# Hybrid encoder layer on one core: block sums, token loads and residual adds are queued in other places

## The chip, the cores and the metric

The kernel is one program on one core of a Trainium2 chip. The metric is the device time of one execution in microseconds (us). The median of three runs before the change is 2272.96 us (2271.06 to 2276.23).

## What is computed

One inference step of a hybrid encoder layer, for 2048 prompt tokens and 32 sample tokens, all in float32, with 1024 model columns and 4096 hidden columns:

```
n = rmsnorm(x);  z = n @ w_in                        # one combined projection
A = windowed attention with sinks, 8 query heads     # half of the width
B = gated linear attention (GLA), 4 heads            # other half
h = x + concat(A, B) @ w_out
y = h + relu(rmsnorm(h) @ w_up)^2 @ w_down
```

It returns y and the new caches and states.

## The kernel before

The program runs four stages one after the other: attention (to about 375 us), GLA (to about 705 us), the output projection (to about 912 us) and the feed-forward part (FFN, to the end). Every float32 operand of a matmul is split into a high and a low part (names end in h and l), and each product of two splits is three matmuls. SyncE (SP) issues all DMAs; each engine works off its own list of instructions in order, and a recording layer with an estimated clock sets that order when the program is built. Generators that are spawned beside a stage (`spawn`) take their places in it by the numbers that they yield, in ns of that clock.

**FFN.** The tokens lie in three pieces of two groups each (328 columns a group in piece 0, 356 in pieces 1 and 2), taken in the order 1, 2, 0 (`ORDER`). A piece is done in 16 blocks of 256 hidden columns. Up and down projections use Strassen-Winograd, so that a block has seven up products (`u`, operands B11, B21, T2, T1, T3, B22, T4) and seven down products (`dn`), which alternate on TensorE. The token operands of a piece are made in the projection stage, stored to memory (`Td`), and loaded by `load_tok` (L1487) when the piece before has used that operand for the last time, about one operand in 3.9 us. `load_tok` loads float32 into the low tile (names T1l and so on), ScalarE copies it to the high tile (T1h), and VectorE or GpSimd subtracts. After each up product ScalarE and VectorE make the operands of the down products (uB11, uB22, uT1, ..., each h and l). `post` of a down product, in `down` (L1569), adds it from PSUM to the accumulators `P` of that piece (VectorE, L1496). Before the first block `residual` (L1606) loads h (`yd`) into accumulators 2, 3, 4 and 5, so that the first block adds onto it as well; accumulators 1, 6 and 7 are written by ScalarE copies. At a piece's end GpSimd merges accumulators (L1594), SP stores them to `out_yT`, and the next piece takes the same tiles. The weights' splits are made up to six steps ahead (`AHEAD`) from tiles named stage, which rotate in a pool of five.

**Block sums of w_down.** The FFN needs, for each of the 16 blocks, four sums of quarters of w_down (`sd`). GpSimd makes them beforehand (L712): blocks 0 to 3 beside attention (in 16 units of 128 columns, in two generators), blocks 4 to 9 beside GLA (1 MB each, in one tile), the rest in the projection by `begin`, `more` and `end`. `down_sums` (L721) loads a unit, yields 6000, sums with a pause after each sum, yields 6000 and stores.

**Output projection.** It goes over six groups (piece, half) in order, loads the residual x of a group as y (`load_y`, pools opy0 to opy2 by turns), loads the mixed heads as m and splits them into mx0 (h by ScalarE, l by GpSimd, L1113), adds (L1271), keeps a sum of squares (`acc`, matmul `oprb`), and hands the group to `post` (L1191), whose two parts run during the next group at f = 1 and 2 (for the last group, inside the FFN's first up products). `post` scales the group, for the second half also forms the Winograd sums T1 to T4, and stores all to Td.

Of the kernel before, what the change touches and what calls it, by code (L numbers as in the profile page):

```python
# [9 lines left out]
F32 = mybir.dt.float32  # L10
F32R = mybir.dt.float32r
I32 = mybir.dt.int32
AF = mybir.ActivationFunctionType
ALU = mybir.AluOpType
# [5 lines left out]
P = 128  # L20
# [6 lines left out]
ORDER = (1, 2, 0)  # L27
EARLY, MIDDLE = 4, 6
AHEAD = 6
# [33 lines left out]
class Builder:  # L63
# [230 lines left out]
    def attention_phase(self):  # L294
# [3 lines left out]
        with ExitStack() as ctx:  # L298
# [337 lines left out]
            for i, t in enumerate(order):  # L636
# [13 lines left out]
                if i == 3:  # L650
                    early = [(b, c0, P) for b in range(EARLY) for c0 in range(0, 512, P)]
                    one = lambda name: self.mid.tile([P, 576], F32, tag="cc", name=name)
                    for j in range(2):
                        self.spawn(self.down_sums(early[j::2], one, 1, 3500), 13000 * j)
                if t == nt - 1:
# [65 lines left out]
    def down_sums(self, units, tile_, parts, step):  # L721

        for b, c0, n in units:
            raw = tile_(f"sd{b}_{c0}")[:, : 4 * n].rearrange("p (k m n) -> p k m n", k=2, m=2)
            self.load_block(raw, b, c0, n)
            yield 6000
            for _ in self.block_sums(raw, parts):
                yield step
            yield 6000
            with self.tc.issue_after(self.Q.last.ins):  # L730
                self.Q.dma_start(self.sd[b][:, :, c0 : c0 + n], raw.rearrange("p k m n -> p (k m) n"))

    def prepare_gla(self, part):
# [66 lines left out]
    def gla_phase(self):  # L800
        tc, a, V, S, G, Q = self.tc, self.a, self.V, self.S, self.G, self.Q
        nt = self.nt
        with ExitStack() as ctx:
# [274 lines left out]
            whole = lambda name: sums.tile([P, 2048], F32, tag="sd", name=name)  # L1078
            self.spawn(self.down_sums([(b, 0, 512) for b in range(EARLY, EARLY + MIDDLE)], whole, 2, 4500), 4000)
            for _ in gates(0):  # L1080
# [76 lines left out]
    def op_phase(self, pool):  # L1157
# [6 lines left out]
        mmem = [[m0.tile([P, KB * REST], F32R, tag=x, name=f"mx0{x}") for x in "hl"], mem1]  # L1164
        yps = [pool(f"opy{i}", 1) for i in range(3)]
        tp, sp, xp = pool("opt", 1), pool("ops", 2), pool("opx", 2)
        stage = lambda name, n: tp.tile([P, H * REST], F32, tag="t", name=name)[:, : H * n].rearrange("p (k t) -> p k t", k=H)
# [23 lines left out]
        def post(p, gi, acc, t3):  # L1191
# [17 lines left out]
            if gi == 0:  # L1209
                for f in range(KB):  # L1210
                    scaled(y[:, f], f)
                    if f == H - 1:
                        Q.dma_start(Td["B11"], y[:, :H])
                Q.dma_start(Td["B21"], y[:, H:])
                return
# [3 lines left out]
            for k in range(H):  # L1219
# [6 lines left out]
                S.activation(y0[:, k], B, AF.Copy)  # L1226
                tt(y0[:, H + k], y0[:, H + k], B)
            for x, src in (("T2", y0[:, :H]), ("T4", y0[:, H:]), ("T1", y[:, :H]), ("T3", t3), ("B22", y[:, H:])):
                Q.dma_start(Td[x], src)
# [11 lines left out]
        def begin(b):  # L1241

            x = xp.tile([P, 2048], F32, tag="x", name=f"sd{b}").rearrange("p (k m n) -> p k m n", k=2, m=2)
            self.load_block(x, b, 0, 512)
            sums[b] = x, self.block_sums(x)
# [12 lines left out]
        for j, (p, gi) in enumerate(groups):  # L1258
# [3 lines left out]
            for f in range(KB):  # L1262
# [18 lines left out]
                if f == KB - 1:  # L1281
                    if gi:
                        Q.dma_start(self.yd[p][gi][:, :H], z)
                    Q.dma_start(self.yd[p][gi][:, H:], y[:, H:])
                if f in (1, 2) and pending is not None:
                    next(pending, None)
# [9 lines left out]
    def ffn_phase(self):  # L1296
# [4 lines left out]
        with ExitStack() as ctx:  # L1301
# [18 lines left out]
            umem |= {x: upair(uc, x) for x in ("T1", "T3", "T2", "B21")}  # L1320
            amem = {1: mem(pool("acc1"), H * NM, "P1", F32)}
            tmem |= tok(pool("tokd"), ("B11", "B21"))
            wfc = pool("wfc")
            amem |= {i: mem(pool(f"acc{i}"), H * NM, f"P{i}", F32) for i in (3, 5, 7, 6, 2, 4)}
            umem["T4"] = upair(pool("ud"), "T4")
            wfb, xa, sx = pool("wfb"), pool("xa", bufs=2), pool("sx")
# [160 lines left out]
            def load_tok(e, x, engs):  # L1487

                h, l = e.T[x]
                Q.dma_start(f32(l), self.Td[e.p][x])  # L1490
                for i, eng in enumerate(engs):
# [77 lines left out]
            def down(g, i):  # L1569
# [7 lines left out]
                for j in range(0, H, 2):  # L1577
# [5 lines left out]
                    for d in to:  # L1583
                        at = e.acc[d][:, j : j + 2]
                        if b or q not in (1, 6, 7):
                            add(at, at, ps)
                        else:
                            S.activation(at, ps, AF.Copy)

# [6 lines left out]
            def store(e, q):  # L1596

                gi, f0 = {2: (0, 0), 3: (1, 0), 4: (0, H), 5: (1, H)}[q]
                for f in range(H):
                    rows, off = slice((f0 + f) * P, (f0 + f + 1) * P), 0  # L1600
                    for t, t0, t1 in e.joined[gi]:
                        dst = self.o["yT_sample"][rows] if t == nt else self.o["yT_prompt"][rows, t0:t1]
                        Q.dma_start(dst, e.acc[q][:, f, off : off + t1 - t0])
                        off += t1 - t0

            def residual(g, i):  # L1606

                n, b = divmod(g, NF)
                if b or i not in (0, 1, 4, 5):
                    return  # L1610
                q = DOWN[i + 1][2]
                gi, f0 = {2: (0, 0), 3: (1, 0), 4: (0, H), 5: (1, H)}[q]
                Q.dma_start(envs[n].acc[q], self.yd[envs[n].p][gi][:, f0 : f0 + H])

# [5 lines left out]
            for x, g, i in steps:  # L1620
# [6 lines left out]
                else:  # L1627
                    residual(g, i)
                    down(g, i)
                    n, b = divmod(g, NF)  # L1630
                    e, end = envs[n], n + 1 == len(envs)
                    if b == NF - 2 and i == 2:
                        merge(e, 3, 5, False)
# [147 lines left out]
```

## Time and profile before

| | |
|---|---|
| median of 3 runs | 2272.96 us |
| the profiled execution | 2273.91 us, span 2272.1 us |
| TensorE busy | 2150.4 us (95%) |
| VectorE, ScalarE, GpSimd busy | 1560.5, 1231.3, 1433.5 us |
| DMA | 372.65 MB, mean 164 GB/s over the span |
| granted TensorE clock, mean | 0.972 |

TensorE is idle for 122 us of the span, and the profile's other views tell where: the waits view names the engine and line that ended each idle stretch, the timeline gives single instructions with start and duration, and the critical chain goes back from the end through whatever released each step. "SPq" rows are DMA issues on SP's queue; their duration is that of the issue, not of the transfer.

### The profile page before, as it was taken

The page shows a single profiled execution, that of the slowest core. Times are in us where ns is not written, and L with a number is a line of the kernel's source. Part 1 is how long each engine was busy: PE and PEld are TensorE (multiplying, and loading weights), DVE is VectorE, ACT ScalarE, POOL GpSimd, SP SyncE. Part 2 cuts the span into 40 slices and gives each one's busy share as a digit, 9 for nine tenths or more (in the row PEclk, how much of TensorE's full clock was granted, in tenths as well). Part 3 has the DMA queues.
Part 4 walks back from the last instruction along what each step waited for, and adds up shares of the span by engine and source line. Part 5 has one row for each costly group of instructions (what it writes and reads, how often), then busy time and mean ns, then how long its engine had stood idle before and what let it go on. Part 6 is the DMA issues. An engine that isn't in the chain of part 4 may idle for free.

```text
span 2272.1 us, 40454 instructions
## 1 busy us (share of the span) xinstructions
PE 2150.4 (95%) x14790; PEld 2018.8 (89%) x14790; DVE 1560.5 (69%) x3442; ACT 1231.3 (54%) x2728; POOL 1433.5 (63%) x1292
## 2 busy tenths in 40 slices
PE   7999999999986899699999997999999989999997
PEld 6777777888776899699999997999999979999996
DVE  8766766799984346567777775566666656776677
ACT  4555555656562122565556565655566646666662
POOL 5243345344351652577777789777777887887784
PEclk9999999999999899799999999999999989999998
DMA  7344563325146897633433358344433584344433
GB/s 265 131 156 144 182 221 132 136 73 193 61 160 191 292 324 260 240 128 127 134 126 127 121 181 311 128 129 128 132 123 121 187 283 144 122 142 133 147 109 118
DMA packets 207145, 372.65 MB, mean 164 GB/s; under 512 B 42961, under 2 KB 136450, under 8 KB 201570
## 3 DMA queue, kind: packets, MB, share of 16 engines
q1 hardware_dynamic: 206946, 370.07, 48.7%
q8 instruction: 116, 1.90, 0.3%
q14 instruction: 83, 0.68, 0.1%
HBM read 275.03 MB, written 94.98 MB: 163 GB/s over the span
## 4 chain that ended last, share of the span: by engine, by line
PE 53%; POOL 2%; DVE 2%; DMA 1%; issue 1%; ACT 0%; SPq 0%; POOLq 0%; DVEq 0%; ACTq 0%
PE dn L156 27%; PE u L156 26%; DVE P L1496 1%; POOL P L1594 1%; DMA out_yT_prompt<-P 0%; POOL wf_d0S L1378 0%; DMA T3l<-Td0T 0%; DMA T1l<-Td2T 0%; DVE P L1594 0%; POOL wf_u1S L1378 0%; DVE u L1496 0%; DMA P<-yd 0%; POOL B22l L1494 0%; POOL wf_d15S L1378 0%; POOL T3l L1494 0%
## 5 line engine op out<-in xcount | busy, mean ns | idle before, releaser
L1496 DVE TENSOR_TENSOR P<-P,dn 128x712 f32<-128x712 f32 (+1 forms) x666 | 580.9, 875 | 261.5 <-PE dn L156 227.3
L43 ACT ACTIVATE u<-u 128x356 f32<-128x356 f32 (+1 forms) x384 | 174.2, 454 | 37.3 <-PE u L156 23.5
L43 ACT ACTIVATE r<-u 128x356 f32<-128x356 f32 (+1 forms) x192 | 88.5, 461 | 138.5 <-PE u L156 138.5
L712 POOL TENSOR_TENSOR sd<-sd 128x128 f32<-128x128 f32 (+2 forms) x136 | 107.0, 806 | 88.4 <-DMA sd<-in_w_down 83.8
L1496 DVE TENSOR_TENSOR u<-u,r 128x356 f32<-128x356 f32 (+1 forms) x144 | 75.7, 525 | 121.5 <-PE u L156 103.1
L944 POOL TENSOR_TENSOR E<-cc 128x256 f32<-128x256 f32 (+1 forms) x117 | 69.5, 629 | 105.7 <-DVE cc L796 52.7
L1403 POOL TENSOR_TENSOR stage<-stage 128x512 f32<-128x512 f32 x92 | 119.3, 1297 | 23.8 <-DMA stage<-in_w_up 17.3
L1020 DVE COPY_PREDICATED AT<-masks,A 64x64 f32<-64x64 int32 (+1 forms) x330 | 82.7, 252 | 18.5 <-ACT AT L43 8.8
L1594 POOL TENSOR_TENSOR P<-P,P 128x712 f32<-128x712 f32 (+1 forms) x38 | 65.2, 1752 | 21.8 <-DVE P L1496 21.6
L43 ACT ACTIVATE P<-S,negm 128x192 f32<-128x192 f32 (+2 forms) x128 | 51.5, 416 | 47.8 <-DVE negm L577 36.7
L1271 DVE TENSOR_TENSOR y<-op,y 128x356 f32<-128x356 f32 (+1 forms) x48 | 23.6, 516 | 74.8 <-PE op L156 63.0
L43 ACT ACTIVATE E<-E 128x1024 f32<-128x1024 f32 (+2 forms) x68 | 67.2, 1012 | 1.1
L595 POOL TENSOR_TENSOR P<-P,es 128x512 f32<-128x512 f32 x15 | 15.6, 1043 | 77.2 <-ACT sq L43 33.8
L43 ACT ACTIVATE v<-go 128x256 f32<-128x256 f32 (+1 forms) x34 | 12.8, 380 | 75.7 <-DVE Sp L1052 44.5
L955 DVE TENSOR_TENSOR E<-E,kq 128x256 f32<-128x256 f32 (+1 forms) x117 | 51.4, 491 | 1.4 <-ACT E L43 1.4
L576 DVE TENSOR_REDUCE mx<-S 128x2 f32<-128x384 f32 (+2 forms) x64 | 32.7, 535 | 28.1 <-PE S L156 27.8
L43 ACT ACTIVATE op<-y 128x356 f32<-128x356 f32 (+1 forms) x42 | 18.7, 463 | 61.1 <-DVE y L1271 61.0
L1496 DVE TENSOR_TENSOR u<-u,f 128x356 f32<-128x356 f32 (+1 forms) x96 | 49.8, 519 | 2.0 <-ACT u L43 2.0
L43 ACT ACTIVATE pS<-pT 128x256 f32<-128x256 f32 (+1 forms) x62 | 27.2, 490 | 43.8 <-PE pT L160 43.8
L844 POOL TENSOR_TENSOR g<-g,ggla 128x512 f32<-128x512 f32 (+1 forms) x17 | 22.6, 1344 | 40.3 <-ACT g L43 40.3
L43 ACT ACTIVATE f<-u 128x356 f32<-128x356 f32 (+1 forms) x96 | 43.7, 455 | 0.0
L156 PEld LDWEIGHTS A<-E 64*64 64x64 f32 (+1 forms) x1704 | 32.5, 147 | 6.7 <-issue 4.7
(1911 smaller groups left out, 8756.6 us busy)
## 6 DMA issues: line engine op xcount, KB each, us to landing
stage<-sd SPq DMA_DIRECT2D x92, 512.0 KB, 4.5
stage<-in_w_up SPq DMA_DIRECT2D x92, 512.0 KB, 4.2
stage<-in_w_down SPq DMA_DIRECT2D x46, 512.0 KB, 3.6
stage<-su SPq DMA_DIRECT2D x30, 512.0 KB, 3.3
sd<-in_w_down SPq DMA_DIRECT2D x24, 512.0 KB, 6.1
sd<-sd SPq DMA_DIRECT2D x12, 1024.0 KB, 7.6
stage<-in_w_down SPq DMA_DIRECT2D x46, 256.0 KB, 3.0
xT1a<-in_xT_prompt SPq DMA_DIRECT2D x16, 512.0 KB, 4.3
```

Source lines behind the costliest of these rows:

```text
L43: ins = f(*args, **kw)
L156: self._pe(self.T.matmul(out, lhsT, rhs, start=start, stop=stop, **kw), ns)
L576: V.reduce_max(mx[:, ch, us], sp, axis=AX.X)
L712: self.G.tensor_tensor(out=o, in0=x, in1=y, op=op)
L844: G.tensor_tensor(out=gv, in0=gv, in1=ggla[:r].unsqueeze(1).broadcast_to([r, 4, P]), op=ALU.mult)
L944: G.tensor_tensor(out=e4, in0=c4, in1=ref, op=ALU.subtract)
L955: V.tensor_tensor(out=e4, in0=e4, in1=halves_of(kq, L, m), op=ALU.mult)
L1020: V.copy_predicated(dst, mk.unsqueeze(1).broadcast_to([L // nh, 2, w // m, m]), src[r].rearrange("s p (n m) -> s p n m", m=m),)
L1271: V.tensor_tensor(out=y[:, f], in0=ps, in1=y[:, f], op=ALU.add)
L1403: tt = lambda o, x, y, op: G.tensor_tensor(out=o, in0=x, in1=y, op=op)
L1496: add = lambda out, x, y, op=ALU.add: V.tensor_tensor(out=out, in0=x, in1=y, op=op)
L1594: eng.tensor_tensor(out=e.acc[q][:, j : j + 2], in0=e.acc[q][:, j : j + 2], in1=e.acc[x][:, j : j + 2], op=ALU.add)
```

## The change

- `EARLY, MIDDLE` goes from 4, 6 to 5, 5: five blocks' sums are made beside attention and five beside GLA. Their pauses are 2500 for 3500 and 3500 for 4500, the second generator starts at 14000 for 13000, and after a unit's store `down_sums` yields 8000 before it loads the next one.
- In the projection the pool opx (sums) has three larger tiles instead of two, and opy0, the pool of the first group's y, is reserved after it, so that it lies over other memory: that of GLA's sums tile.
- `post` yields once more before it stores to Td, so that the stores come some steps later.
- `load_tok` issues its DMA from ScalarE's queue instead of SP's.
- The first block no longer adds onto a loaded h in accumulators 2 to 5: VectorE copies the product there (L1592 of the changed kernel). h comes later: in blocks 2 to 9 of each piece one slice of 128x712 is loaded into a stage tile and GpSimd adds it after VectorE's own add of that block.
- The FFN's memory pools stand in another order.

```diff
-EARLY, MIDDLE = 4, 6
+EARLY, MIDDLE = 5, 5
...
             with self.tc.issue_after(self.Q.last.ins):
                 self.Q.dma_start(self.sd[b][:, :, c0 : c0 + n], raw.rearrange("p k m n -> p (k m) n"))
+            yield 8000
...
-        yps = [pool(f"opy{i}", 1) for i in range(3)]
-        tp, sp, xp = pool("opt", 1), pool("ops", 2), pool("opx", 2)
+        yps = [pool(f"opy{i}", 1) for i in (1, 2)]
+        tp, sp, xp = pool("opt", 1), pool("ops", 2), pool("opx", 3)
+        yps.insert(0, pool("opy0", 1))
...
-                    if f == H - 1:
-                        Q.dma_start(Td["B11"], y[:, :H])
+                yield
+                Q.dma_start(Td["B11"], y[:, :H])
                 Q.dma_start(Td["B21"], y[:, H:])
...
                 tt(y0[:, H + k], y0[:, H + k], B)
+            yield
             for x, src in (("T2", y0[:, :H]), ("T4", y0[:, H:]), ("T1", y[:, :H]), ("T3", t3), ("B22", y[:, H:])):
...
-                if f in (1, 2) and pending is not None:
+                if f in (1, 2, 4 if gi else 6) and pending is not None:
                     next(pending, None)
...
                 h, l = e.T[x]
-                Q.dma_start(f32(l), self.Td[e.p][x])
+                S.dma_start(f32(l), self.Td[e.p][x])
...
-                        if b or q not in (1, 6, 7):
+                        if b:
                             add(at, at, ps)
+                        elif q in (1, 6, 7):
+                            S.activation(at, ps, AF.Copy)
                         else:
-                            S.activation(at, ps, AF.Copy)
+                            V.tensor_copy(at, ps)
...
+            rest = [(q, gi, f) for q, gi, f0 in ((3, 1, 0), (5, 1, H), (2, 0, 0), (4, 0, H)) for f in (f0, f0 + 2)]
+            waiting = {}
             def residual(g, i):
                 n, b = divmod(g, NF)
-                if b or i not in (0, 1, 4, 5):
+                e = envs[n]
+                if not 2 <= b < 2 + len(rest):
                     return
-                q = DOWN[i + 1][2]
-                gi, f0 = {2: (0, 0), 3: (1, 0), 4: (0, H), 5: (1, H)}[q]
-                Q.dma_start(envs[n].acc[q], self.yd[envs[n].p][gi][:, f0 : f0 + H])
+                q, gi, f = rest[b - 2]
+                if i == 0:
+                    waiting[g] = load(self.yd[e.p][gi][:, f : f + 2])
+                if DOWN[i][2] == q:
+                    at = e.acc[q][:, f % H : f % H + 2]
+                    G.tensor_tensor(out=at, in0=at, in1=waiting.pop(g), op=ALU.add)
```

The order of TensorE's instructions stays as it was. On ScalarE, at the change from piece 2 to piece 0 (about 1805 to 1825 us), the list was this; T2l, T1l and T3l are token operands loaded by SP, u are up products on their way to the operands uB22 and uT1 of the last down products.

```order
L43 ACTIVATE B21h<-B21l 128x656 x2
L43 ACTIVATE r_10728<-u_1_20025 128x356
L43 ACTIVATE wf_u15A_20177<-stage 128x512
L43 ACTIVATE T2h<-T2l 128x656 x2
L43 ACTIVATE r_10729<-u_3_20158 128x356
L43 ACTIVATE T1h<-T1l 128x656 x2
L43 ACTIVATE u_0_20219<-u_0_20219 128x356
L43 ACTIVATE uB22h<-u_0_20219 128x356
```

At the same place it is this now.

```order
L43 ACTIVATE B21h<-B21l 128x656 x2
L43 DMA T2l<-Td0T_192 128x1312
L43 ACTIVATE r_10748<-u_1_20085 128x356
L43 ACTIVATE wf_u15A_20237<-stage 128x512
L43 ACTIVATE T2h<-T2l 128x656 x2
L43 DMA T1l<-Td0T_193 128x1312
L43 ACTIVATE r_10749<-u_3_20218 128x356
L43 ACTIVATE T1h<-T1l 128x656 x2
L43 DMA T3l<-Td0T_194 128x1312
L43 ACTIVATE u_0_20279<-u_0_20279 128x356
L43 ACTIVATE uB22h<-u_0_20279 128x356
```

The work of ScalarE is the same, but the load of an operand now stands behind the copy of the operand before it.

On VectorE at the FFN's start (about 944 to 960 us) the list was this; dn_3 and dn_5 are the second and third down product, and P their accumulators.

```order
L1218 TENSOR_TENSOR y_9863<-y_9863,opb 128x356
L1378 TENSOR_TENSOR wf_d0A_11211<-stage,wf_d0A_11211 128x512
L1496 TENSOR_TENSOR u_2_11172<-u_2_11172,r_10727 128x356
L1496 TENSOR_TENSOR uB11l<-u_2_11172,uB11h 128x356
L1496 TENSOR_TENSOR P_10785<-P_10785,dn_3_0_11151 128x712
L1496 TENSOR_TENSOR P_10785<-P_10785,dn_3_2_11159 128x712
```

Now it is this.

```order
L1220 TENSOR_TENSOR y_9883<-y_9883,opb 128x356
L1592 COPY P_10798<-dn_3_0_11169 128x712
L1592 COPY P_10798<-dn_3_2_11177 128x712
L1380 TENSOR_TENSOR wf_d0A_11229<-stage,wf_d0A_11229 128x512
L1498 TENSOR_TENSOR u_2_11190<-u_2_11190,r_10747 128x356
```

The copies of dn_3 stand ahead of three instructions that the adds stood behind. On SP, at the projection's start (706 to 729 us), the list was this; y_9180 is the y of the first group, y_9194 that of the second, y_9243 that of the third, and sd_144 is GLA's store of a block's sums.

```order
L59 DMA mixT_81<-gT_9046 128x512
L59 DMA sd_144<-sd_0_8511 128x2048
L59 DMA y_9194<-in_xT_prompt 128x8x112
L59 DMA y_9243<-in_xT_prompt 128x8x16
L59 DMA y_9243<-in_xT_prompt 128x8x128 x2
L59 DMA y_9243<-in_xT_prompt 128x8x84
L59 DMA y_9180<-in_xT_prompt 128x8x128 x2
L59 DMA y_9180<-in_xT_prompt 128x8x40
L59 DMA y_9180<-in_xT_sample 128x8x32
```

Now it is this, where y_9200, y_9214 and y_9263 are the first, second and third group's.

```order
L59 DMA mixT_81<-gT_9080 128x512
L59 DMA sd_145<-sd_0_8552 128x2048
L59 DMA y_9263<-in_xT_prompt 128x8x128
L59 DMA y_9263<-in_xT_prompt 128x8x84
L59 DMA y_9214<-in_xT_prompt 128x8x88
L59 DMA y_9214<-in_xT_prompt 128x8x128
L59 DMA y_9214<-in_xT_prompt 128x8x112
L59 DMA m_112_9316<-mixT_70 128x8x16
L59 DMA m_0_9320<-mixT_71 128x1024
L59 DMA y_9200<-in_xT_prompt 128x8x128 x2
L59 DMA y_9200<-in_xT_prompt 128x8x40
L59 DMA y_9200<-in_xT_sample 128x8x32
```

The first group's y is still the last of the three. Between the store of the sums and it stood 468 columns of y (a column is 4 KB), and now 540 columns of y and 144 of m.

More of the change, by code (lines that the diff above doesn't have):

```diff
@@ L653, in attention_phase @@
                     for j in range(2):
-                        self.spawn(self.down_sums(early[j::2], one, 1, 3500), 13000 * j)
+                        self.spawn(self.down_sums(early[j::2], one, 1, 2500), 14000 * j)
                 if t == nt - 1:
@@ L1078, in gla_phase @@
             whole = lambda name: sums.tile([P, 2048], F32, tag="sd", name=name)
-            self.spawn(self.down_sums([(b, 0, 512) for b in range(EARLY, EARLY + MIDDLE)], whole, 2, 4500), 4000)
+            self.spawn(self.down_sums([(b, 0, 512) for b in range(EARLY, EARLY + MIDDLE)], whole, 2, 3500), 4000)
             for _ in gates(0):
@@ L1241, in begin @@
         def begin(b):
-            x = xp.tile([P, 2048], F32, tag="x", name=f"sd{b}").rearrange("p (k m n) -> p k m n", k=2, m=2)
+            x = xp.tile([P, 2592], F32, tag="x", name=f"sd{b}")[:, :2048].rearrange("p (k m n) -> p k m n", k=2, m=2)
             self.load_block(x, b, 0, 512)
@@ L1320, in ffn_phase @@
             umem |= {x: upair(uc, x) for x in ("T1", "T3", "T2", "B21")}
-            amem = {1: mem(pool("acc1"), H * NM, "P1", F32)}
             tmem |= tok(pool("tokd"), ("B11", "B21"))
+            amem = {i: mem(pool(f"acc{i}"), H * NM, f"P{i}", F32) for i in (3, 5, 7, 6, 2, 4, 1)}
+            umem["T4"] = upair(pool("ud"), "T4")
             wfc = pool("wfc")
-            amem |= {i: mem(pool(f"acc{i}"), H * NM, f"P{i}", F32) for i in (3, 5, 7, 6, 2, 4)}
-            umem["T4"] = upair(pool("ud"), "T4")
             wfb, xa, sx = pool("wfb"), pool("xa", bufs=2), pool("sx")
@@ L1627, in ffn_phase @@
                 else:
-                    residual(g, i)
                     down(g, i)
@@ L1631, in ffn_phase @@
                     e, end = envs[n], n + 1 == len(envs)
+                    residual(g, i)
+                    if g == i == 0:
+                        next(self.pending, None)
                     if b == NF - 2 and i == 2:
```

## The prediction

> **What bounds the kernel now.** I read the page first, then the table of windows, then TensorE's waits, and then single places in the timeline and the critical chain. The page's first part gives the busy time of each engine.
>
> ```profile
> PE 2150.4 (95%) x14790; PEld 2018.8 (89%) x14790; DVE 1560.5 (69%) x3442; ACT 1231.3 (54%) x2728; POOL 1433.5 (63%) x1292
> ```
>
> TensorE is busy 2150.4 of 2272.1 us. The change leaves its instructions and their order alone, so only the 122 us in which it idles, and its clock, can move. The windows' columns are the window, then busy us of PE, PEld, DVE, ACT and POOL, granted clock, DMA share and GB/s.
>
> ```profile
> 720.00:740.00 20.00, 4.95 (x34) 4.71 (x32) 9.73 (x18) 3.85 (x10) 6.01 (x7) 0.70 1.07 322
> 1100.00:1300.00 200.00, 200.00 (x1229) 200.00 (x1229) 147.52 (x217) 119.70 (x253) 147.15 (x116) 1.00 0.39 129
> ```
>
> In the steady FFN (second row) TensorE never idles, GpSimd has 53 of 200 us free and DMA runs at 129 GB/s. The first row is the projection's start, where TensorE stands and DMA is full. TensorE's waits in 700 to 960 us and in 1300 to 1900 us (total, times, longest) give the other places.
>
> ```profile
> PE oprb L156 <- issue: 15.1, 1, 15.1
> PE dn L156 <- DVE y L1218: 11.8, 1, 11.8
> PE op L156 <- POOL mx0l L1113: 4.6, 1, 4.6
> PE dn L156 <- DVE P L1496: 4.0, 1, 4.0
> PE op L156 <- DVE y L1271: 3.5, 1, 3.5
> ...
> PE dn L156 <- DVE P L1496: 17.7, 5, 7.0
> ```
>
> The 17.7 us of the last row are the two changes of piece, mostly. There the edits on h and on the token loads act, one each way.
>
> **The residual at the changes of piece.** At the first change the end of the longest wait reads so (SP, POOL, DVE, PE).
>
> ```profile
> 1413.34 0.32 SPq L59 DMA_DIRECT2D P<-yd  x1
> 1413.61 2.59 POOL L1378 TENSOR_TENSOR wf_d0S<-stage,wf_d0S 128x512 fp32r<-128x512 f32 x2
> 1417.44 1.70 DVE L1496 TENSOR_TENSOR P<-P,dn 128x712 f32<-128x712 f32 x2 [5.01 <-POOL wf_d0A L1378]
> 1418.48 0.64 PE L156 MATMUL dn<-uT3h,wf_d0S 128*128 128x356 f32 x1 [6.95 <-DVE P L1496]
> ```
>
> h is loaded at 1413.34, when the stores of the last piece have landed, and the add can start 4.1 us later. A copy needs the stores alone, so it could start at 1413.34. Then the next limit is the weight split of GpSimd, whose first half ends at about 1414.9. So 1418.48 becomes about 1415, 3.5 us earlier. At the second change the critical chain itself holds the load.
>
> ```profile
> 1866.53 4.03 DMA P<-yd
> ...
> 1871.58 3.46 PE dn L156 x12
> ```
>
> Here the 4.03 us go as they stand. The product behind the wait takes 3.46 us, where the steady window has 1.97 (200 us for 1229 matmuls, so 12 in 1.95): the clock is low after a long idle. A shorter wait saves up to 1 us of that.
>
> **The token loads.** In the changed list of ScalarE the load of T1 stands behind the copy of T2, and that of T3 behind the copy of T1. Each copy waits until its own load has landed, so three round trips come one after the other. Before, SP issued each as soon as TensorE had let go of the tile. Second change, SP and then ScalarE.
>
> ```profile
> 1800.24 0.32 SPq L59 DMA_DIRECT2D B21l<-Td0B  x1
> ...
> 1804.17 0.32 SPq L59 DMA_DIRECT2D T2l<-Td0T  x1
> ...
> 1808.09 0.32 SPq L59 DMA_DIRECT2D T1l<-Td0T  x1
> ...
> 1812.01 0.32 SPq L59 DMA_DIRECT2D T3l<-Td0T  x1
> ```
>
> ```profile
> 1801.87 1.40 ACT L43 ACTIVATE B11h<-B11l 128x656 fp32r<-128x656 f32 x2 [2.72 <-DMA B11l<-Td0B]
> ...
> 1805.67 1.38 ACT L43 ACTIVATE B21h<-B21l 128x656 fp32r<-128x656 f32 x2
> ...
> 1809.32 1.40 ACT L43 ACTIVATE T2h<-T2l 128x656 fp32r<-128x656 f32 x2 [1.39 <-DMA T2l<-Td0T]
> ...
> 1812.51 1.39 ACT L43 ACTIVATE T1h<-T1l 128x656 fp32r<-128x656 f32 x2 [1.44 <-DMA T1l<-Td0T]
> ...
> 1819.67 1.39 ACT L43 ACTIVATE T3h<-T3l 128x656 fp32r<-128x656 f32 x2 [2.08 <-DMA T3l<-Td0T]
> 1820.97 0.45 ACT L43 ACTIVATE uT1h<-u 128x356 fp32r<-128x356 f32 x1
> ```
>
> With the same transfer times: if B21's copy stays where it is, T2l is issued at 1807.1 (+2.9), lands 5.1 us later, its copy ends at 1813.6; T1l is issued then (+5.5), takes 4.4, its copy ends at 1819.4; T3l is issued then (+7.4) and takes 7.6. So uT1h, which stands behind T3's copy, comes 7.4 us later. B21l itself now stands behind B11's copy (1803.3 for 1800.24), which makes up to 10; if T3l lands as quickly as T1l (4.4 us), it is 4. What waits for uT1h is VectorE, and behind it the accumulator adds, and TensorE.
>
> ```profile
> 1822.77 2.50 DVE L1496 TENSOR_TENSOR P<-P,dn 128x712 f32<-128x712 f32 x3
> ...
> 1824.72 0.40 PE L156 MATMUL dn<-uB22h,wf_d15S 128*128 128x356 f32 x1 [1.02 <-DVE P L1496]
> ```
>
> The adds at 1822.77 stand right behind uT1l and uT3l, and TensorE waited for them already. So nothing covers the delay: the product at 1824.72 starts 4 to 10 us later, I take 8 (between +7.4 and +10). The chain of stores that ends at 1871.58 hangs on TensorE's products in between, so it moves along, less the 4.03 us: +4 for the second change, bounds −4 (nothing late) and +8.
>
> At the first change the same holds with smaller numbers and more cover.
>
> ```profile
> 1351.80 0.32 SPq L59 DMA_DIRECT2D T1l<-Td2T  x1
> ...
> 1353.81 1.49 ACT L43 ACTIVATE T2h<-T2l 128x712 fp32r<-128x712 f32 x2 [2.12 <-DMA T2l<-Td2T]
> ...
> 1357.38 1.49 ACT L43 ACTIVATE T1h<-T1l 128x712 fp32r<-128x712 f32 x2 [1.73 <-DMA T1l<-Td2T]
> ...
> 1371.56 0.59 PE L156 MATMUL dn<-uB22h,wf_d15S 128*128 128x356 f32 x2 [1.87 <-POOL wf_d15S L1378]
> ```
>
> T1l is issued at 1355.3 (T2's copy's end) for 1351.80, its copy ends at 1362.4 for 1358.9, and T3l follows that. Operands behind T3's copy come some 6 us later, but TensorE stood until 1371.56 for GpSimd, so about 4 us reach it, and the wait of 6.95 us before 1418.48 takes most of those in. So the first change comes out at −3.5, +4 less 2.5 taken in: −2, bounds −5 and +3. Longer idle before 1824.72 and 1371.56 costs half-clock time as at 1871.58, about 1.5 us each, less the 1 us saved: +1.5 in all.
>
> The Trainium skill ("DMA: Bandwidth & Descriptors", Issuing engines are not separate DMA queues) says that DMAs from different engines run on the same 16 DMA engines, and that another issuing engine only saves the sequencer's time. By it the new queue can give back no more than the issues' 0.32 us each, and the sum would stand without any gain in transfer time, which is how I made it.
>
> **The FFN's start.** ScalarE, TensorE, and VectorE:
>
> ```profile
> 912.53 0.63 ACT L43 ACTIVATE wf_u0S<-stage 128x512 fp32r<-128x512 f32 x1 [2.89 <-PE op L156]
> ...
> 914.69 0.40 PE L156 MATMUL u<-B11h,wf_u0A 128*128 128x356 f32 x1 [2.20 <-issue]
> ...
> 954.14 0.69 DVE L1378 TENSOR_TENSOR wf_d0A<-stage,wf_d0A 128x512 fp32r<-128x512 f32 x1 [8.98 <-ACT wf_d0A L43]
> ...
> 958.22 1.70 DVE L1496 TENSOR_TENSOR P<-P,dn 128x712 f32<-128x712 f32 x2
> ```
>
> B11 was loaded long before. Its load now stands on ScalarE behind wf_u0S, which waits for the projection's end at 912.5: issued at 913.2, landed after some 4.1 to 4.8 us (T1l and T2l above were 4.4 and 5.1), copied at about 918.9 instead of before 912. So the first product starts 4.2 us later, and the 11.8-us wait, which ends when VectorE has done the last group's post, moves along, since that post waits for a matmul behind that product. On the other side the copies of dn_3 stand ahead of wf_d0A, so that they run before 954.14 instead of at 958.22; the 4.0-us wait goes. Together 0, bounds −4 and +5.
>
> **Projection, GLA, attention.** VectorE, then TensorE, at the projection's start:
>
> ```profile
> 728.96 3.37 DVE L1271 TENSOR_TENSOR y<-op,y 128x328 f32<-128x328 f32 x8 [4.71 <-DMA y<-in_xT_sample]
> ...
> 738.76 1.25 PE L156 MATMUL oprb<-ones,acc 128*82 128x1 f32 x8 [15.05 <-issue]
> ```
>
> VectorE waited until the first group's y had landed at 728.9, and TensorE went on 9.8 us behind that. Ahead of it stand 216 columns of 4 KB more (0.89 MB): at 322 GB/s that is +2.8 us, and nothing covers it. One GpSimd sum of 512 columns (1.3 us, half of the two splits of that size at 1413.61) falls between the splits of mx0, whose end ends the 4.6-us wait: +1.3. The 3.5-us wait for y at L1271 goes, since the loads of that group stand earlier and the sums' store ahead of them is done: −3. Together +1, bounds −3 and +6. In attention, TensorE waited once for GpSimd.
>
> ```profile
> PE pT L160 <- POOL P L595: 1.3, 1, 1.3
> ```
>
> GpSimd waited for w_down there; four more units with longer pauses may end that or move it: −1, bounds −2 and +1. In GLA one block less is summed, but sums fall beside other tiles, and that costs:
>
> ```profile
> 570.11 7.21 DVE L928 TENSOR_TENSOR Qc<-kq,ec 128x256 f32<-128x256 f32 x1
> ```
>
> A 128x256 operation of VectorE took 7.21 us while GpSimd ran E and the sums back to back. That may vanish or come up elsewhere: +1, bounds −4 and +5.
>
> **The adds of h.** GpSimd adds 24 slices of 128x712.
>
> ```profile
> L1594 POOL TENSOR_TENSOR P<-P,P 128x712 f32<-128x712 f32 (+1 forms) x38 | 65.2, 1752 | 21.8 <-DVE P L1496 21.6
> ```
>
> At 1.75 us each they are 42 us, one in a block of 27 us that leaves GpSimd 7 us free: 0. Their loads add 8.8 MB at a time when DMA is at 129 GB/s, in exchange for the same bytes at the full changes of piece.
>
> **Sum.** −2 + 4 + 1.5 + 0 + 1 + 1 − 1 = +4.5 on the profiled execution of 2273.91 us, which lies 0.95 above the median: 2278.4, of which I make 2278 in the runs. A measurement of this kernel can tell about 0.2% (4.5 us) from no change; 2278 lies 5 us above the median.
>
> **Rivals.** (1) Faster: the token loads' round trips are hidden. If the loads come back in 2 to 3 us once SP's queue no longer stands ahead of them, or TensorE's other products cover the lag, the second change gives −4, the first −3.5, the clock −1, and the rest as above (0 + 1 + 1 − 1): −7.5, which is 2265.5 from the median. For it speaks that the loads of h leave the full stretch; against it that B11l took 4 us before the stretch was full. Chance 0.27. (1b) The same, and the projection's start and GLA gain as well (their lower bounds, −4 and −5 more): about 2256. Chance 0.08. (2) No change: the delay of ScalarE is about half of what I think, or the chain to 1871.58 hangs on stores and GpSimd, not on TensorE: 2269 to 2277. Chance 0.24. (3) The Trainium skill's page "SBUF — State Buffer" (Who interferes with whom) says that a VectorE operation with two SBUF inputs is fully blocked while GpSimd reads SBUF. As a mechanism here, the 24 adds would stop VectorE's splits (wf_d0A above) for 1.75 us each, as Qc was stopped, and if TensorE felt each, it would be +42 us, 2320. Against it: in the steady window GpSimd is busy 147 us, and TensorE lost nothing. By that rule Qc's 7.21 us agree, the steady window shows that it reaches no end. Chance 0.01. The forecast, slower by 5 to 15 us, has 0.40.
>
> **How the numbers follow.** Faster by over 0.2%: 0.27 + 0.08 = 0.35. Within: 0.24. Slower: 0.41. Cases of both signs hold most of the chance; the forecast's own range is 2274 to 2288. The whole range reaches to rival 1 and leaves out 1b and the outer part of the forecast: 2262 to 2288.
>
> **What would show it.** Right: at the second change T1l and T3l are issued from ScalarE 5 to 10 us after TensorE has left the tile, and TensorE's wait before dn<-uB22h, 1.02 us now, is 5 us or more; the first u<-B11h starts 6 us after the projection's last matmul; no P<-yd is left and the products after the stores wait for copies. Wrong: T3's copy still ends within 8 us of T1's, and the waits at both changes together fall by more than 5 us. The first group's y should land 3 us later than now, measured from mixT's last store.

## The result, and the profile after

The changed kernel takes 2294.09 us (median of 10 runs, 2283.52 to 2298.4) against 2276.19 for the kernel before on the same chips: a ratio of 1.0076 [1.0056, 1.0095], slower by some 17 us. (One of the ten runs before, at 2638.71 us, was in a slow state and is left out of the ratio.) The forecast was 2278, slower, with a range of 2262 to 2288: the sign was right, the size was not. The profiled execution takes 2295.51 us (span 2293.6, clock 0.968). Its busy times are these.

```profile
PE 2155.3 (94%) x14790; PEld 2021.7 (88%) x14790; DVE 1575.3 (69%) x3442; ACT 1232.0 (54%) x2728; POOL 1474.0 (64%) x1324
```

TensorE has the same 14790 matmuls and 4.9 us more busy time; its idle time went from 122 to 138 us. The steady FFN still loses nothing, though GpSimd has 11 us more to do in it; the projection's start, in a window 25 us later than before, still has a TensorE that stands and a full DMA.

```profile
745.00:765.00 20.00, 5.65 (x38) 5.38 (x36) 7.79 (x14) 3.86 (x10) 4.03 (x3) 0.72 1.03 296
1100.00:1300.00 200.00, 200.00 (x1231) 200.00 (x1230) 151.50 (x220) 120.61 (x255) 158.08 (x123) 1.00 0.43 138
```

TensorE's waits of the changed kernel, from three stretches of time (380 to 745, 745 to 1000 and 1300 to 1900 us):

```profile
PE go L156 <- ACT cc L43: 9.8, 1, 9.8
...
PE oprb L156 <- issue: 21.1, 1, 21.1
PE dn L156 <- DVE y L1220: 13.1, 1, 13.1
PE u L156 <- ACT B11h L43: 5.9, 1, 5.9
PE op L156 <- POOL mx0l L1114: 5.8, 1, 5.8
...
PE dn L156 <- DVE P L1498: 12.9, 4, 6.2
```

The first row is new: a wait of 9.8 us in GLA, where I had seen nothing. The wait for oprb grew from 15.1 to 21.1, B11h's 5.9 is new, mx0l's went from 4.6 to 5.8, and the rows `DVE y L1271` (3.5) and P at the FFN's start (4.0) are gone.

**By stages.** The next table follows a few of TensorE's instructions (by name, the same in each kernel) through the profiled executions. Each number says by how many us a stage became longer (+) or shorter than in the profiled kernel before. GLA's start goes from the kernel's beginning, so with attention, to the first product gTp, the rest of GLA to the last; the projection's start to the first oprb, its rest to the last op; the FFN's start to the first product dn<-uT2 with the weight d0S; a change of piece from that product with d14S to that with d0S of the next piece. The total goes to TensorE's last product; what the stages leave of it lies elsewhere. Stages that an edit doesn't touch differ by up to 4 us, and the rest of GLA by more: e1 and e4 have the same lists of instructions in GLA as the kernel before, and +7.7 and +1.1 there; the changed kernel and e2 differ in the FFN's token loads alone, and have +7.7 and +.5. So only larger numbers, or such as come back in several kernels, are read, and the rest of GLA hardly at all.

| | GLA start | GLA rest | proj. start | proj. rest | FFN start | 1st change | 2nd change | total |
|-|-|-|-|-|-|-|-|-|
| forecast | | +1 | +2.8 | −1.7 | 0 | −2 | +4 | +4.5 |
| after | +19.2 | +7.7 | +6.0 | −4.4 | +2.6 | −4.4 | −4.6 | +21.3 |
| e1 old sums | −.5 | +7.7 | +21.8 | −.3 | +3.9 | −6.6 | −5.3 | +19.4 |
| e2 loads on SP | +22.1 | +.5 | +6.5 | −4.5 | +2.7 | −7.4 | −12.4 | +8.1 |
| e3 new sums alone | +20.3 | +16.6 | +3.3 | +6.4 | +.9 | −.3 | +1.8 | +48.4 |
| e4 old sums, SP | −.4 | +1.1 | +21.5 | −3.8 | +3.7 | −7.4 | −11.2 | +4.2 |
| e5 residual alone | −.1 | −3.9 | +.3 | +.3 | −5.0 | −7.5 | −12.4 | −27.2 |
| e6 e5 + ScalarE loads | +.7 | −1.1 | +1.2 | −.3 | −5.2 | −4.9 | −5.3 | −15.5 |
| e7 e5 + FFN pools | +2.7 | +.5 | +.6 | +.9 | +1.1 | −7.4 | −10.7 | −11.9 |
| e8 no pause | −.4 | +.6 | −14.8 | −3.0 | +1.8 | −7.2 | −5.2 | −29.2 |
| e9 pause early | +23.1 | +8.9 | −15.2 | −2.3 | +2.0 | −7.3 | −5.4 | +2.5 |
| e10 pause in GLA | −1.8 | +5.7 | +6.2 | −4.0 | +2.8 | −7.3 | −5.2 | −4.5 |
| e11 no pause, SP | −.4 | −3.0 | −15.2 | −1.9 | +4.4 | −7.5 | −12.7 | −36.3 |
| e12 e8, timed | −1.5 | +1.9 | −15.2 | −3.9 | +1.6 | −4.7 | −3.8 | −26.2 |

(Forecast: attention's −1 and the clock's +1.5 are in its total alone.) So the loss is in GLA and, by a smaller part, at the projection's start, and the change gained in both changes of piece, where the forecast had −2, +4 and 1.5 of clock, a loss together.

**The new wait in GLA.** ScalarE, SP and TensorE of the changed kernel:

```profile
420.39 0.84 ACT L43 ACTIVATE cc<-la,packed 128x256 f32<-128x256 f32 x2 [12.57 <-DMA sd<-sd]
```

```profile
405.67 1.20 SPq L59 DMA_DIRECT2D sd<-in_w_down  x2
406.91 0.61 SPq L59 DMA_DIRECT2D sd<-sd  x1
...
416.25 1.20 SPq L59 DMA_DIRECT2D sd<-in_w_down  x2
417.71 4.55 SPq L59 DMA_DIRECT2D sd<-sd  x2
```

```profile
421.29 0.63 PE L156 MATMUL go<-Ss,Qc 64*32 64x128 f32 x2 [9.82 <-ACT cc L43]
```

ScalarE wants to write GLA's gates cc for the second group of 256 tokens (they hold the running sums of the decays), and waits 12.57 us for a store of block sums. The units of the sums that are made beside attention (L652, the tag "cc" of the pool mid) rotate through the same two memory slots as cc (L778). In the kernel before, SP stored the last of these units at 349.22, and ScalarE wrote cc without a wait.

```profile
349.22 0.57 SPq L59 DMA_DIRECT2D sd<-sd  x1
```

```profile
402.25 0.82 ACT L43 ACTIVATE cc<-la,packed 128x256 f32<-128x256 f32 x2
```

Now units are still being loaded at 416. The line that delays them is `yield 8000`, the pause after each unit's store.

### The profile page after: what moved, and what is told of

Its sections match the earlier page's. It is cut to its first block, busy times and chain, and to the rows that moved or that the text cites. A ratio compares the mean times of both kernels' runs of the same rounds, so it can differ in the third digit from the quotient of the medians.

```text
span 2293.6 us, 40613 instructions
## 1 busy us (share of the span) xinstructions
PE 2155.3 (94%) x14790; PEld 2021.7 (88%) x14790; DVE 1575.3 (69%) x3442; ACT 1232.0 (54%) x2728; POOL 1474.0 (64%) x1324
## 4 chain that ended last, share of the span: by engine, by line
PE 52%; DMA 2%; DVE 2%; ACT 0%; issue 0%; POOL 0%; SPq 0%; ACTq 0%; DVEq 0%
PE dn L156 26%; PE u L156 26%; DVE P L1498 1%; DMA T3l<-Td2T 0%; DMA T1l<-Td2T 0%; DMA T1l<-Td0T 0%; DMA T2l<-Td0T 0%; DMA T3l<-Td0T 0%; DVE u L1498 0%; DMA B21l<-Td0B 0%; DMA T2l<-Td2T 0%; DVE P L1598 0%; SPq L59 0%; DMA stage<-sd 0%; DMA B11l<-Td2B 0%
## 5 line engine op out<-in xcount | busy, mean ns | idle before, releaser
L1498 DVE TENSOR_TENSOR P<-P,dn 128x712 f32<-128x712 f32 (+1 forms) x642 | 559.7, 875 | 234.5 <-PE dn L156 217.4
L1598 POOL TENSOR_TENSOR P<-P,P 128x712 f32<-128x712 f32 (+1 forms) x38 | 65.0, 1732 | 21.8 <-DVE P L1498 21.6
L595 POOL TENSOR_TENSOR P<-P,es 128x512 f32<-128x512 f32 x15 | 16.0, 1065 | 74.2 <-ACT sq L43 44.4
L845 POOL TENSOR_TENSOR g<-g,ggla 128x512 f32<-128x512 f32 (+1 forms) x17 | 23.1, 1373 | 48.6 <-ACT g L43 48.6
L43 ACT ACTIVATE v<-go 128x256 f32<-128x256 f32 (+1 forms) x34 | 12.7, 380 | 73.5 <-DVE Sp L1053 46.0
L1281 POOL TENSOR_TENSOR z<-y 128x356 f32<-128x356 f32 (+1 forms) x12 | 11.8, 983 | 53.0 <-DVE y L1274 35.0
```

The costliest lines, as they stand in the source:

```text
L43: ins = f(*args, **kw)
L845: G.tensor_tensor(out=gv, in0=gv, in1=ggla[:r].unsqueeze(1).broadcast_to([r, 4, P]), op=ALU.mult)
L1498: add = lambda out, x, y, op=ALU.add: V.tensor_tensor(out=out, in0=x, in1=y, op=op)
L1598: eng.tensor_tensor(out=e.acc[q][:, j : j + 2], in0=e.acc[q][:, j : j + 2], in1=e.acc[x][:, j : j + 2], op=ALU.add)
```

## The experiments

**e1, e2, e3.** I started with two explanations: the sums' new schedule (through the slots of cc), and the loads on ScalarE's queue. e1 takes the schedule of the kernel before into the changed kernel, e2 the queue, e3 puts the new schedule alone into the kernel before.

```diff
# e1, against the changed kernel (e3: the reverse, in the kernel before)
-EARLY, MIDDLE = 5, 5
+EARLY, MIDDLE = 4, 6
-    self.spawn(self.down_sums(early[j::2], one, 1, 2500), 14000 * j)
+    self.spawn(self.down_sums(early[j::2], one, 1, 3500), 13000 * j)
-            yield 8000
-            ... whole, 2, 3500), 4000)
+            ... whole, 2, 4500), 4000)
# e2, against the changed kernel
-                S.dma_start(f32(l), self.Td[e.p][x])
+                Q.dma_start(f32(l), self.Td[e.p][x])
```

> The changed kernel with the block sums as before (4 blocks beside attention, 6 beside GLA, old pauses, no 8000 after a store). Slot theory (the units of w_down sums share the two slots named cc with GLA's gates; in the changed kernel the last units run into GLA, ScalarE's write of cc waits 12.6 us for a store of sums, and GLA loses 23 us, attention 4): ScalarE's wait for the store of sums goes, the first copy of gT lies within 2 us of 439.4, and the time falls by 20 to 30 us, to 2264 to 2274. Queue theory (the token loads on ScalarE's queue are the main loss): the time stays at 2288 to 2295.

Measured: 2287.04 us (2285.54 to 2293.93), 1.0062 [1.0037, 1.0087]. GLA's start is back (−.5), so its loss came with the new schedule. But the total hardly moved, since the projection's start now costs 21.8 us. SP and VectorE of e1 show why.

```profile
742.22 0.33 SPq L59 DMA_DIRECT2D sd<-sd  x1
746.08 2.43 SPq L59 DMA_DIRECT2D y<-in_xT_prompt  x3
748.55 1.52 SPq L59 DMA_DIRECT2D y<-in_xT_sample  x1
```

```profile
753.90 3.37 DVE L1273 TENSOR_TENSOR y<-op,y 128x328 f32<-128x328 f32 x8 [21.69 <-DMA y<-in_xT_sample]
```

The first group's y now lies over the tile of GLA's sums, so its loads can't start before the last store of sums, which six blocks put at 742.22. The old schedule and the new place of y don't fit each other.

> The changed kernel with the token loads issued by SyncE again. Slot theory: the GLA loss stays; only the FFN's start (about 6 us) and the changes of piece (0 to 8 us) gain: 2280 to 2288. Queue theory: 2272 to 2280, and TensorE's waits at both changes of piece fall by 8 us or more.

Measured: 2285.44 us (2279.42 to 2293.73), 1.0056 [1.0037, 1.0075]. Against the changed kernel, the changes of piece moved, the second to −12.4 and the first to −7.4, and the rest of GLA, which no edit of e2 touches. The loss up to GLA's first gTp stays.

> The kernel before with the new block sums alone (5 and 5 blocks, new pauses, 8000 after a store). Slot theory: ScalarE waits over 10 us for a store of sums before cc, the first copy of gT comes 13 to 19 us later than before, and the time is 2295 to 2303. Queue theory: within 5 us of before.

Measured: 2311.6 us (2304.12 to 2323.13), 1.0174 [1.0135, 1.0214]. The schedule alone costs 38 us in the kernel before, more than either theory had. Its profiled execution is the slowest of the four, 49 us over that of the kernel before; 37 us of these lie in GLA, 20.3 of them up to the first gTp. So the schedule is the cause, and other parts of the change gain some 20 us back.

**e4: both at once**, old schedule and loads on SP.

> The changed kernel with old block sums and with SyncE's token loads; the new residual, pools and late Td stores stay. Slot theory: the loss is gone and the residual gains at three places (about 6 at the FFN's start, 4 at each change of piece, less some us at the projection's start): 2258 to 2266. Queue theory: 2258 to 2266 as well, but with e1 near the changed kernel. If the residual itself gains nothing: 2270 to 2278.

Measured: 2277.58 us (2271.02 to 2287.64), 1.0024 [1.0008, 1.004]. By the total alone the residual would have gained nothing, but the stages say otherwise: GLA is whole, the changes of piece gain 7.4 and 11.2 us, and the projection's start costs 21.5, which is y behind the sums' store, as in e1.

**e5, e6, e7: the gain, part by part.** e5 puts the new residual alone (copies in the first block, slices added by GpSimd in blocks 2 to 9) into the kernel before; e6 adds the loads on ScalarE's queue to it, and e7 the new order of the FFN's memory pools instead.

```diff
# e6, against e5
-                Q.dma_start(f32(l), self.Td[e.p][x])
+                S.dma_start(f32(l), self.Td[e.p][x])
# e7, against e5
-            amem = {1: mem(pool("acc1"), H * NM, "P1", F32)}
             tmem |= tok(pool("tokd"), ("B11", "B21"))
+            amem = {i: mem(pool(f"acc{i}"), H * NM, f"P{i}", F32) for i in (3, 5, 7, 6, 2, 4, 1)}
+            umem["T4"] = upair(pool("ud"), "T4")
             wfc = pool("wfc")
-            amem |= {i: mem(pool(f"acc{i}"), H * NM, f"P{i}", F32) for i in (3, 5, 7, 6, 2, 4)}
-            umem["T4"] = upair(pool("ud"), "T4")
```

> The kernel before with the new residual alone (copy in the first block, h added by GpSimd in blocks 2 to 9). From the landmarks of e4, the residual gains 6 us at the FFN's start and 7.5 and 11 at the two changes of piece: 2246 to 2253. If those gains came from the pools' order or from a shifted phase and not from the residual: 2262 to 2270 (3.5 + 4 + 4 as recorded).

Measured: 2246.2 us (2245.07 to 2246.81), 0.9862 [0.9838, 0.9885], 29 us faster on its chip. Of that, 25 us lie in the FFN's start and the two changes. Windows over the changes, of the kernel before and then of e5 (each set from the same products on):

```profile
1340.00:1430.00 90.00, 77.16 (x441) 75.43 (x440) 47.00 (x69) 50.97 (x101) 85.66 (x60) 0.92 0.82 289
1800.00:1880.00 80.00, 69.26 (x410) 68.20 (x409) 41.08 (x62) 42.81 (x88) 71.46 (x50) 0.91 0.83 286
```

```profile
1331.00:1414.00 83.00, 75.09 (x444) 73.35 (x443) 48.01 (x70) 50.12 (x99) 82.63 (x58) 0.98 0.76 265
1784.00:1852.00 68.00, 64.97 (x412) 64.18 (x411) 41.08 (x62) 42.33 (x87) 66.36 (x46) 1.00 0.76 273
```

At the second change TensorE idled 10.7 us and now 3.0; and its 412 matmuls take 64.97 us where 410 took 69.26, as the granted clock is 1.00 and not 0.91. So a shorter idle is paid twice: 7.7 us of waiting and 4.3 of slow matmuls. At the first change it is 4.9 and 2.1. What waits are left there (e5, 1300 to 1900 us) are short.

```profile
PE dn L156 <- POOL wf_d0S L1378: 3.2, 2, 2.0
PE dn L156 <- POOL wf_d15S L1378: 2.8, 2, 2.0
PE dn L156 <- DVE P L1496: 2.5, 2, 1.4
```

> As e5, but with the token loads issued by ScalarE. Queue theory, from the landmarks of the changed kernel against e2: the loads cost 3 to 5 us at the first change of piece, 6 to 8 at the second and nothing at the FFN's start: 8 to 13 us above e5. If the FFN's start loses by the queue as well (B11 behind ScalarE's wait, as recorded), 12 to 18 us above e5.

Measured: 2255.06 us (2251.09 to 2259.11), 0.9902 [0.9879, 0.9926]: the queue costs 8.9 us in the medians of the same chip, 7.1 at the second change and 2.6 at the first. At the FFN's start it costs nothing (−5.2 for −5.0): with the old pools ScalarE issues B11's load at 881.33, long before it is needed.

> As e5, but with the FFN's memory pools in the new order. If it is the pools' order that lets B11's load start only when the projection has ended (e2 and e4 lose 9 us there with SyncE's loads too), 5 to 10 us above e5, with the first product on B11 5 us after the projection's last; if the late Td stores or something else does it, as e5.

Measured: 2256.02 us (2251.54 to 2262.16), 0.9908 [0.988, 0.9937]: the pools cost 9.8 us in the medians, of which the table finds 6.1 at the FFN's start and 1.7 at the second change. SP's load of B11, in e5 and then in e7, and TensorE's wait for it in e7:

```profile
877.32 1.05 SPq L59 DMA_DIRECT2D B11l<-Td1B  x1
```

```profile
917.17 0.32 SPq L59 DMA_DIRECT2D B11l<-Td1B  x1
```

```profile
PE u L156 <- ACT B11h L43: 5.1, 1, 5.1
```

The load goes out when the projection has ended: SP waits 14.3 us for TensorE's products op ahead of it. As the pools alone were changed, I take it that B11 now lies over memory that these products read to the end; the load then waits for it on whichever queue it is issued.

**e8, e9, e10: the pause alone.** e8 is the changed kernel without `yield 8000`; e9 keeps the pause only in the units beside attention, e10 only in those beside GLA. Each is one execution.

```diff
# e8
-            yield 8000
# e9 (e10: parts == 2)
-            yield 8000
+            if parts == 1:
+                yield 8000
```

> The changed kernel without the 8000 after a store of sums. Slot theory: the units come sooner, so that fewer or none hold a slot when GLA writes cc; ScalarE's wait for the store falls below 4 us and the first copy of gT comes 3 to 8 us after that of before instead of 19. If the loss lies in the fifth block itself (GpSimd's or the DMA's share) and not in when the slots come free, the first gT stays 15 us or more late.

Measured: 2245.12 us. ScalarE writes cc at 401.97 without a wait, GLA costs nothing, and the projection's start is 14.8 us shorter than in the kernel before. SP of e8:

```profile
674.12 0.42 SPq L59 DMA_DIRECT2D sd<-sd  x1
679.31 3.19 SPq L59 DMA_DIRECT2D y<-in_xT_prompt  x3
682.54 3.04 SPq L59 DMA_DIRECT2D y<-in_xT_sample  x1
```

With five blocks and no pause the last store of sums is out at 674, so the first group's y, right behind it, lands while GLA still runs. In the changed kernel the same rows are these.

```profile
735.63 0.43 SPq L59 DMA_DIRECT2D sd<-sd  x1
...
749.19 3.75 SPq L59 DMA_DIRECT2D y<-in_xT_prompt  x3
752.98 1.62 SPq L59 DMA_DIRECT2D y<-in_xT_sample  x1
```

> The changed kernel with the 8000 after a store only in the units beside attention. Slot theory: these units hold the slots of cc into GLA's start, so ScalarE still waits some 12 us for a store of sums and the first copy of gT is 17 to 20 us late, but nothing more is lost in GLA, and the projection's first y no longer waits: 2258 to 2270. If GLA's start is lost by something else (GpSimd's order, SP's queue) that the pause in GLA's own units brings, the first gT is on time.

Measured: 2277.08 us. ScalarE of e9:

```profile
425.38 0.84 ACT L43 ACTIVATE cc<-la,packed 128x256 f32<-128x256 f32 x2 [13.81 <-DMA sd<-sd]
```

The wait for the slot is back, GLA's start costs 23.1 us, and the rest of GLA 8.9, which with the 3 us more at its start puts the time over the range; the projection's start keeps its gain of 15.2.

> The changed kernel with the 8000 only in the units beside GLA. Slot theory: the first gT on time; the later units run up to the projection, so the GLA's second half loses 5 to 8 us and the first group's y, which lies in the memory of the sums' tile, waits for the last store: first oprb 5 to 20 us later than without the pause: 2255 to 2272.

Measured: 2269.54 us. GLA starts on time, its rest costs 5.7 us (less than the 7.7 that e1 shows there without any pause), and the projection's start costs 6.2, as in the changed kernel. So the pause costs twice, at two places: some 20 us up to GLA's first gTp, by the units beside attention (+19.2 and +23.1 with their pause, −1.8 to −.4 without), and about 21 us at the projection's start, by the units beside GLA (+6.0 and +6.2 with theirs, −14.8 to −15.2 without).

That the second goes through the tile under y is read from the rows: in e8 SP waits 3.1 us for the store and sends y as it lands; in e1 y goes out right behind the late store. In the changed kernel the store of 735.63 has landed at 743.4, and y, which stands behind it and behind other loads on SP, goes out at 749.19. The changed kernel with y over other memory was not run.

**e11, e12: the best version.** e12 is e8 run several times; e11 also has the token loads back on SP.

> The kernel of e8 once more, timed: 2242 to 2250, ratio to the kernel before 0.985 to 0.990, that is, the pause alone costs 45 to 50 us. If e8 was a lucky single run: 2255 or more.

Measured: 2247.81 us (2244.91 to 2249.09), 0.9896 [0.9869, 0.9924]. The changed kernel stands at 1.0076, so the pause alone costs 1.8%, 41 us, which is the 20 and the 21 above.

> The changed kernel without the pause and with SyncE's token loads. By e6 against e5 the queue costs 9 us, so 9 us below e8: 2234 to 2240. If the queue's cost hides behind the later start of B11 in this pool order: 2240 to 2246.

Measured: 2244.79 us (2238.23 to 2246.05), 0.9879 [0.9853, 0.9905]: faster than both kernels. Its interval overlaps those of e12 and e5, so which of the three is best stays open. It gained 3 us on e12 and not the 9 of the queue in e5 and e6. Its profile has the second change at −12.7 for −3.8 in e12, but is of its fastest run, 6.6 us under its median. The FFN's old pools were not tried with it.

## Why the prediction was right and wrong

**GLA: the step that failed.** "In GLA one block less is summed, but sums fall beside other tiles, and that costs: ... +1, bounds −4 and +5." With attention, for which I put −1, it was +26.9: 19.2 up to the first gTp and 7.7 after it. The wait for the slots of cc, 9.8 us of TensorE's time, stood nowhere in the sum. I had followed the orders of instructions and the bytes of the DMAs, and asked which engine the sums run beside. I had not asked what memory a unit holds while it pauses, and who takes that memory next. Ten units in each generator, each 8 us longer on the planner's clock, run past attention's end, and the slot of cc comes free with a store. e8 to e10 show it by the pause alone. That it is the slot, and not the longer run of sums beside GLA, rests on ScalarE's row (12.57 us behind a store of sums; 13.81 in e9; none in e8 and e10); cc in memory of its own was not run.

The other 9.4 of the 19.2 us lie on both sides of that wait. About 5 came before it; in attention TensorE's wait for GpSimd's P (L595) grew from 1.3 to 4.4 us. About 4 came behind it: the products from there to the first gTp take 36.8 us for 32.8, at a granted clock of 0.75 for 0.84. The 7.7 after the first gTp are no sure cost of the pause. The VectorE operation Qc that took 7.21 us in the kernel before takes as long at another place of the changed kernel, and some 20 us later TensorE waits 3.9 us for VectorE; in e2, whose lists of instructions in GLA are the same, the Qc of that place is short, and the wait is 1.4 us (changed kernel, then e2).

```profile
516.82 7.08 DVE L929 TENSOR_TENSOR Qc<-kq,ec 128x256 f32<-128x256 f32 x1
```

```profile
519.68 0.62 DVE L929 TENSOR_TENSOR Qc<-kq,ec 128x256 f32<-128x256 f32 x1
```

So this mechanism I had right ("That may vanish or come up elsewhere"), and the same list can have it or not in one execution.

**The projection's start.** I put y at +2.8. From mixT's last store to y's landing it was 20.9 us and is 22.9: +2.0, nearly as forecast. The other 4.0 of the +6.0 come after the landing.

```profile
757.91 3.37 DVE L1274 TENSOR_TENSOR y<-op,y 128x328 f32<-128x328 f32 x8 [5.99 <-DMA y<-in_xT_sample]
761.20 10.43 DVE L1277 TENSOR_TENSOR acc<-acc,op 128x328 f32<-128x328 f32 x8
```

```profile
760.82 16.99 POOL L712 TENSOR_TENSOR sd<-sd 128x512 f32<-128x512 f32 x12 [31.36 <-DMA sd<-in_w_down]
```

VectorE's eight adds to acc start with GpSimd's sums and take 1.3 us each, for 0.5 alone. What I missed outright is the other side: without the pause this stage is 15 us shorter than before. Rival 1b had this gain, at 4 us. The 3.5-us wait at L1271 went, and mx0l's grew by 1.2, both as forecast; the rest of the projection gained 2 us more than these two, which nothing here explains.

**The residual.** I put −4.03 at the second change and −3.5 at the first, and 1 us of clock; e5 has −12.4 and −7.5. The steps were right (the loads of h go, GpSimd's splits are next), the sizes were not: I took the longest piece of the chain, 4.03, for the whole saving, though all of the second wait (6.25 us, dn<-uT3h at 1871.58) hung on it and the next limit was not close behind, and I priced the clock at 1 us where it was 4.3 and 2.1. (The clock's term was also added wrongly: 1.5 twice less 1 is 2, not 1.5.) GpSimd's 24 adds are covered, as forecast: TensorE is busy 200.00 of 200 us beside them, so rival 3 is out.

**The queue.** I put +8 at the second change and +4 less 2.5 at the first; e6 has +7.1 and +2.6. ScalarE of the changed kernel shows the round trips in series.

```profile
1833.82 0.33 ACTq L43 DMA_DIRECT2D T2l<-Td0T  x1
1840.42 0.75 ACT L43 ACTIVATE T2h<-T2l 128x656 fp32r<-128x656 f32 x1 [4.38 <-DMA T2l<-Td0T]
1840.42 0.35 ACTq L43 DMA_DIRECT2D T1l<-Td0T  x1
...
1847.95 0.76 ACT L43 ACTIVATE T1h<-T1l 128x656 fp32r<-128x656 f32 x1 [5.79 <-DMA T1l<-Td0T]
1847.96 0.36 ACTq L43 DMA_DIRECT2D T3l<-Td0T  x1
```

Each load goes out when the copy of the load before it is let go, and ScalarE then waits for it again. The test that I gave was partly wrong: the lag shows in front of dn<-uB22h at the first change (6.20 us), while at the second it is spread over several products, and the last product of block 15 starts 6.3 us late. The sign of being wrong that I gave for T3 could not tell the cases apart: its copy ends 5.6 us after T1's, within the 8 us, though both are late. The Trainium skill ("DMA: Bandwidth & Descriptors", Issuing engines are not separate DMA queues) says that another issuing engine saves the sequencer's time only. The trace agrees as far as it goes: e6 shows no gain anywhere. Its loss of 8.9 us comes from the order on ScalarE, but not from that alone: from issue to landing the loads of T2 and T1 took 7.3 and 6.9 us there, for 4.9 and 5.5 in e5. The prediction had taken the same times for both; why they grew stays open.

**The FFN's start.** The forecast 0 came out at +2.6, but one of its two steps was wrong. "Its load now stands on ScalarE behind wf_u0S": true, and TensorE did wait 5.9 us for B11h; but e6 and e7 show that the pools' order makes the load late, and that the queue does not. P's 4.0-us wait went, as forecast, and shows as −5.0 in e5.

**The sum.** By the runs: residual −29, queue +9, FFN's pools +10, pause +41, and for the rest (five and five blocks, y over the sums' tile, later stores) what is missing to +17, some −14, which fits the −15.2 of e12 at the projection's start. That the parts add up is assumed: in e11 the queue's part was 3, not 9. Without the pause, my sign would have been wrong.

## What to carry to other kernels

A pause in a helper that runs beside the main work is not free time: it lengthens how long the helper holds its memory, so list who takes each slot or address next, and when, before the pause is priced. When a tile moves over memory of another, its loads hang on the last user of that memory; the order of the DMA queue doesn't show that. And when a stall goes, add the slow matmuls behind it to the saving, from the windows' clock. Before a stage's number is put down to an edit, see how far it moves between kernels that are the same there; here one stage moved by 7 us.

## What the runs showed of the hardware

With 10.7 us of idle in the 80 us of the second change, TensorE's granted clock was 0.91; with 3.0 us it was 1.00, and that gain in the matmuls (4.3 us) is over half of the gain in waiting (7.7 us).

VectorE's adds of 128x328 with both inputs in SBUF (acc, at the projection's start) took nearly as long as the GpSimd sum that they ran beside. In the kernel before, single instructions of VectorE and then of GpSimd read so.

```profile
733.25 0.50 DVE L1274 TENSOR_TENSOR acc<-acc,op 128x328 f32<-128x328 f32 x1
736.35 0.83 DVE L1274 TENSOR_TENSOR acc<-acc,op 128x328 f32<-128x328 f32 x1
737.29 1.37 DVE L1274 TENSOR_TENSOR acc<-acc,op 128x328 f32<-128x328 f32 x1
```

```profile
735.85 0.98 POOL L712 TENSOR_TENSOR sd<-sd 128x256 f32<-128x256 f32 x1
736.79 1.51 POOL L712 TENSOR_TENSOR sd<-sd 128x512 f32<-128x512 f32 x1
739.21 0.72 POOL L712 TENSOR_TENSOR sd<-sd 128x256 f32<-128x256 f32 x1
739.89 1.27 POOL L712 TENSOR_TENSOR sd<-sd 128x512 f32<-128x512 f32 x1
```

An add takes 0.50 us alone, 0.83 beside a sum of 256 columns and 1.37 beside one of 512; the sums take 0.98 and 1.51 beside adds, and 0.72 and 1.27 alone. In the changed kernel all the sums there have 512 columns, and six of the eight adds take 1.37 to 1.38. The Trainium skill ("SBUF — State Buffer", Who interferes with whom) says that such a VectorE operation contends with GpSimd's reads; the rows agree. In these rows one sum goes with one add, so that wider GpSimd operations make VectorE's small ones dearer. That is no rule: the Qc of 7.21 us in the kernel before stood while GpSimd ran four operations on E and six sums one after the other.
